# Which rows are kept, where raw weights lie and when gathers begin in a two-layer encoder with a product-key expert layer

## The chip, the cores and the metric

The kernel runs on one core of a Trainium2 chip. The metric is device time in microseconds of one execution; runs of a kernel are told as their median. The profile is of one execution, taken by the hardware profiler.

## The reference, cut

Two layers act on 512 tokens of width 1024. Each layer has a mixing part (retention and dilated attention), a cross-attention to 256 memory tokens, and an expert layer. Only the expert layer is touched by the change:

```python
def block(xb):                                   # 128 tokens
    q = (xb @ w_query).reshape(128, 8, 2, 128)
    half_scores = jnp.einsum('thcd,ckd->thck', q, keys_f)          # 2 x 128 keys a head
    top_s, top_i = lax.top_k(half_scores, 16)
    cand_s = top_s[:, :, 0, :, None] + top_s[:, :, 1, None, :]
    cand_i = top_i[:, :, 0, :, None] * 128 + top_i[:, :, 1, None, :]
    best_s, best_pos = lax.top_k(cand_s.reshape(128, 8, -1), 16)
    expert_idx = jnp.take_along_axis(cand_i.reshape(128, 8, -1), best_pos, axis=-1)
    gates = jax.nn.softmax(best_s, axis=-1)
    u, v = expert_down[expert_idx], expert_up[expert_idx]          # 16384 experts of width 1024
    act = jax.nn.gelu(jnp.einsum('thkd,td->thk', u, xb))
    return jnp.einsum('thk,thkd->td', gates * act, v)
```

So each token uses 8 x 16 = 128 of 16384 experts. All is in float32.

## The kernel before

The 512 tokens are four blocks of 128, numbered 0 to 3. The kernel computes the expert layer in two ways. For blocks 0 to 2 (`ND` = 384 tokens) it is *dense*: all 16384 experts are multiplied out, and a gate array `Gd` in DRAM, zero where an expert wasn't chosen, selects. For block 3 it is *sparse*: the 128 rows that each token chose are gathered from DRAM, one slot for all 128 tokens at a time.

The dense part goes over 128 groups (`i1`) of 128 experts. `Dense.down` loads a group's down weights into a `w_raw` tile (512 KB, on the queue of SyncE, SP), splits it into a high part `w_hi` (ScalarE, line 106) and a low part `w_lo` (VectorE, line 107), does 24 matmuls of 128 x 384 into the PSUM tile `pj` (line 658; 8 steps of three products of the parts), and ScalarE writes the gelu of it as a tile `c`. `up_parts` loads the group's up weights in the same way, multiplies `c` with the gates (VectorE, line 688) and splits it into `ch` and `cl`; `up` does 18 matmuls of 128 x 512 (line 700) into six accumulators that fill six banks of PSUM for the whole stage. `w_raw` has four tiles (`WR`) for both kinds of weights.

The sparse part issues an indirect DMA on GpSimd's queue for each of 128 slots (line 560), first from the down table, where VectorE takes a dot product of each row with the token (line 565), then from the up table, where VectorE adds the weighted row to `x` (line 571). A gathered tile is 512 KB, and `RB` = 3 of them exist.

A `Route` object holds a block's choice: `sv` and `si` are the top-16 scores and indices of each half (written by `top16` in `tail`, while the query projection runs), `half` combines them for four heads (VectorE mostly; ScalarE's exponential in it is line 793), `gates` builds one-hot rows (VectorE, lines 836 to 850), multiplies them on TensorE (lines 859 and 860) and writes `Gd`. Tiles of Routes 0 and 2 share names (`sv0`), and so a buffer; Route 1 has `sv1`, and Route 3 has a set of its own in the pool `layer`.

`layer` writes the order of the program with generators. For the expert layer it is:

1. Eight steps, each with one piece of the second pair's query projection (`t1`), three steps of the choices of Routes 0 and 1, and two downs whose `c` is put away in DRAM (`Cd`), since the PSUM that the ups need is still in use. Such blocks are the *kept* ones.
2. The rest of the choices of Routes 0, 1 and 2, with two downs a step, then downs until `LAG` = 60 are kept (blocks 0 to 59).
3. `rest`: blocks 60 to 127, each with its down and its up; after each, the ups of as many kept blocks as fall due, whose `c` is read back as `cd` (three tiles). Gate tiles are loaded eight blocks at a time (1536 KB), as `gt` for the blocks with a down and as `gtb` for the kept ones, two tiles each. Beside it run Route 3's two halves and the 256 gathers, 262 steps spread over the 68 blocks.

This program order is then handed to a scheduler (`schedule_with_timeline_sim`), which sets each engine's order and the waits; each engine and each queue works in that order.

Of the kernel before, what the change touches and what calls it, by code (L numbers as in the profile page):

```python
# [8 lines left out]
F32 = mybir.dt.float32  # L9
# [12 lines left out]
D = 1024  # L22
# [5 lines left out]
NK = 128  # L28
NE = NK * NK
SLOTS = 128  # L30
# [5 lines left out]
GSC = 4096.0  # L36
ND = 384
# [15 lines left out]
WR = 4  # L53
KH = 7
AH = 5
FP = ((0, 0, 0), (0, 1, 1))
SIDE = 262


class Kernel:  # L60
# [67 lines left out]

    def wload(self, src):
        raw = self.wp.tile([128, D], F32, name="w_raw", bufs=WR)  # L130
        self.nc.sync.dma_start(raw if len(src.shape) == 2 else raw.rearrange("p (a b) -> p a b", a=src.shape[1]), src)
        return raw

    def wsplit(self, src, pool=None):

        raw = self.wload(src)
# [307 lines left out]
    def tail(self, l, pair, pools, gp, lp):  # L444

        nc, a, ps = self.nc, self.a, self.ps
        sb = pools["tail"]
# [7 lines left out]
        hT = operand(FP[pair][0], "P_lo")  # L455
# [49 lines left out]
        self.bcast_rows(gain, a["norm_ffn"], l * D, D)  # L505
        d = 2 * pair * 128
        inner = d + 256 <= ND
        if inner:
            hT = [t[:, :, d:d + 256] for t in self.hT]
        else:  # L510
            hT = pools["hq"].tile([128, KT, 256], F32, name="hq"),
        keep = {}
        for i in range(2):
            b = 2 * pair + i
            if b * 128 >= ND:
                keep[i] = self.hn[b] = lp.tile([128, D], F32, name=f"hn{b}")
        for i, h in self.norm_rows(sb, xs, gain, keep, ("a4", A4)):
            b = 2 * pair + i
            self.to_T(h, hT, i * 128, self.hT if b * 128 < ND and not inner else None, b * 128)
        yield  # L520
# [30 lines left out]

    def sparse(self, b, r, gp, lp):
        nc, a = self.nc, self.a
        ei = r.ei
        act = lp.tile([128, SLOTS], F32, name=f"act{b}")
        c = lp.tile([128, SLOTS], F32, name=f"cf{b}")

        def gather(tab, j):
            t = gp.tile([128, D], F32, name="row", bufs=RB)
            nc.gpsimd.indirect_dma_start(out=t, out_offset=None, in_=tab,  # L560
                                         in_offset=bass.IndirectOffsetOnAxis(ap=ei[:, j:j + 1], axis=0))
            return t
        for j in range(SLOTS):
            t = gather(a["expert_down"], j)
            nc.vector.scalar_tensor_tensor(t, t, 1.0, self.hn[b], op0=OP.mult, op1=OP.mult, accum_out=act[:, j:j + 1])  # L565
            yield
        nc.scalar.activation(c, act, AF.Gelu_apprx_tanh)
        nc.vector.tensor_mul(c, c, r.g)
        for j in range(SLOTS):
            t = gather(a["expert_up"], j)  # L570
            nc.vector.scalar_tensor_tensor(self.x[b], t, c[:, j:j + 1], self.x[b], op0=OP.mult, op1=OP.add)  # L571
            yield

    def layer(self, l):
        nc, a = self.nc, self.a
        with ExitStack() as lst:
# [3 lines left out]
            dp = self.pool(lst, "gdram", space=DRAM)  # L580
            self.hn, self.routes = {}, []
            self.Gd = dp.tile([ND // TB, 128, NK, TB], F32, name="Gd")
# [31 lines left out]
            def sparse():  # L614
                for r in self.routes:
                    if r.b * 128 >= ND:
                        r.sb = late
                        yield from r.half(0)
                        yield from r.half(1)
                        r.rows(lp)  # L620
                        yield from self.sparse(r.b, r, late, lp)
            dense.rest(late, sparse())

# [10 lines left out]
class Dense:  # L634
# [3 lines left out]
    def __init__(self, k, l, sb, dp):  # L638
        self.k, self.l, self.sb = k, l, sb
        self.nb = ND // 128  # L640
        self.gview = k.Gd.rearrange("n p i t -> p n i t")
        self.Cd = dp.tile([LAG, 128, ND], F32, name="Cd")
        self.acc, self.started = {}, set()
        self.n = 0
# [19 lines left out]
    def ahead(self, n):  # L664

        for i1 in range(self.n, min(self.n + n, LAG)):
            self.k.nc.scalar.dma_start(self.Cd[i1], self.down(i1))
            self.n = i1 + 1

    def kept(self, i1):  # L670
        c = self.late.tile([128, ND], F32, name="cd", bufs=3)
        self.k.nc.sync.dma_start(c, self.Cd[i1])
        return c

    def gates(self, pool, i1, name, bufs):

        if i1 % GI == 0 or name not in self.gt:
            t = self.gt[name] = pool.tile([128, ND // TB, GI, TB], F32, name=name, bufs=bufs)
            i0 = i1 // GI * GI
            self.k.nc.sync.dma_start(t, self.gview[:, :, i0:i0 + GI, :])  # L680
        return self.gt[name][:, :, i1 % GI, :]

# [20 lines left out]

    def rest(self, pool, side):

        k, nb = self.k, self.nb
        for b in range(nb):
            self.bank(b)
        self.gt, self.late = {}, pool
        owed = 0.0  # L710
        kept = 0
        last = []

        def add(parts, i):
            if i < NK - 2:
                self.up(parts, 0, nb)
            else:
                last.append(parts)
        n = 0
        for i1 in range(LAG, NK):  # L720
            add(self.up_parts(self.down(i1), self.gates(pool, i1, "gt", 2), i1), n)
            n += 1
            while kept < LAG and kept * (NK - LAG) < (i1 + 1 - LAG) * LAG:
                add(self.up_parts(self.kept(kept), self.gates(pool, kept, "gtb", 2), kept), n)
                kept += 1
                n += 1
            owed += SIDE / (NK - LAG)
            take(side, int(owed))
            owed -= int(owed)
        take(side, 1000)  # L730
        for b in range(nb):
            self.up(last[0], b, b + 1)
            self.up(last[1], b, b + 1, True)
            for h in range(2):
                x = k.x[b][:, h * 512:(h + 1) * 512]
                k.nc.vector.tensor_add(x, self.acc[b, h], x)


class Route:


    def __init__(self, k, l, b, sb, lp):
        self.k, self.l, self.b, self.sb = k, l, b, sb
        i = b % 2
        if b * 128 >= ND:
# [59 lines left out]
    def rows(self, lp):  # L805

        self.ei = lp.tile([128, SLOTS], I32, name=f"ei{self.b}")
        self.k.nc.vector.tensor_scalar(self.ei, self.ef, float(self.l * NE), None, op0=OP.add)

    def gates(self):  # L810
# [18 lines left out]
        def pairs(x, t, n):  # L829

            return x[:, t:t + n].rearrange("p (o t) -> p o t", t=TP)[:, :, None]

        def same(out, j, t):
            n, m = out.shape[1] * TP, out.shape[2]
            v = [128, n // TP, m, TP]
            nc.vector.tensor_tensor(out, k.iota_r[:, None, 0:m, :].to_broadcast(v), pairs(iT[:, j], t, n).to_broadcast(v),
                                    op=OP.is_equal)
        no = OB // TP
        for t0 in range(0, 128, OB):
# [11 lines left out]
            for t1 in range(0, OB, TB):  # L851
# [3 lines left out]
                for q in range(0, TB, 4):  # L855
# [5 lines left out]
                    nc.scalar.activation(stage[:, :, q:q + 4], pg.rearrange("p t i -> p i t"), AF.Copy, scale=1.0 / GSC)  # L861
                nc.scalar.dma_start(k.Gd[(self.b * 128 + t0 + t1) // TB], stage)
# [62 lines left out]
```

## Time and profile before

| | |
|---|---|
| median of 3 runs | 3653.78 us (3647.8 to 3661.69) |
| the profiled execution | 3647.1 us, span 3645.3 us |
| TensorE (PE) busy | 3501.8 us, 96% |
| VectorE (DVE) busy | 2651.4 us, 73% |
| ScalarE (ACT) busy | 1481.2 us, 41% |
| GpSimd (POOL) busy | 640.9 us, 18% |
| DMA, mean over the span | 848.42 MB, 233 GB/s |

Layer one's `rest` runs from about 965 to 1822 us of the span, layer two's from about 2786 to 3626. The rows of a table by stretches give, after the stretch and its length, the busy time of PE, PE's weight loads (PEld), DVE, ACT and POOL with the number of instructions in brackets, then the clock that TensorE was granted (1.00 is full), the busy share of the 16 DMA engines, and GB/s. A row of waits says who stood idle at which line for whom: total us, times, longest. "SPq" is SyncE's DMA queue; q1 in the list of queues is that queue, q10 ScalarE's, q0 GpSimd's. Matmuls overlap in the pipeline, so that the time from one start to the next, and not the duration of one, is what a matmul costs.

### The profile page before, as it was taken

The page shows a single profiled execution, that of the slowest core. Times are in us where ns is not written, and L with a number is a line of the kernel's source. Part 1 is how long each engine was busy: PE and PEld are TensorE (multiplying, and loading weights), DVE is VectorE, ACT ScalarE, POOL GpSimd, SP SyncE. Part 2 cuts the span into 40 slices and gives each one's busy share as a digit, 9 for nine tenths or more (in the row PEclk, how much of TensorE's full clock was granted, in tenths as well). Part 3 has the DMA queues.
Part 4 walks back from the last instruction along what each step waited for, and adds up shares of the span by engine and source line. Part 5 has one row for each costly group of instructions (what it writes and reads, how often), then busy time and mean ns, then how long its engine had stood idle before and what let it go on. Part 6 is the DMA issues. An engine that isn't in the chain of part 4 may idle for free.

```text
span 3645.3 us, 55355 instructions
## 1 busy us (share of the span) xinstructions
PE 3501.8 (96%) x20844; PEld 3190.9 (88%) x20844; DVE 2651.4 (73%) x5818; ACT 1481.2 (41%) x2214; POOL 640.9 (18%) x518
## 2 busy tenths in 40 slices
PE   8999999999899999999989999999998999999997
PEld 7989989999788888888779899899997888888886
DVE  5565559976677777878855655599766777878787
ACT  4453544454433333333333535345544333333332
POOL 0000000000133433434300000000000333333342
PEclk9999999999999999999999999999999999999998
DMA  5242444666799989998832434346668999999986
GB/s 158 77 135 94 152 127 148 221 227 229 250 318 326 331 313 325 332 320 308 306 96 77 129 105 152 122 150 219 230 226 253 333 329 327 328 325 338 325 311 237
DMA packets 432252, 848.42 MB, mean 233 GB/s; under 512 B 27888, under 2 KB 282864, under 8 KB 425840
## 3 DMA queue, kind: packets, MB, share of 16 engines
q1 hardware_dynamic: 326384, 489.89, 41.2%
q0 software_dynamic: 73728, 268.47, 20.8%
q10 hardware_dynamic: 31872, 86.52, 6.6%
q8 instruction: 163, 2.67, 0.3%
q14 instruction: 105, 0.86, 0.1%
HBM read 756.17 MB, written 76.02 MB: 228 GB/s over the span
## 4 chain that ended last, share of the span: by engine, by line
PE 55%; issue 14%; DMA 12%; DVE 9%; POOL 7%; ACT 2%; SPq 1%; POOLq 0%; DVEq 0%; ACTq 0%
PE pj L658 16%; PE pj L167 13%; PE pj L183 9%; DMA row<-in_expert_up,ei 7%; POOL row L560 7%; PE s L700 2%; PE t L700 2%; DVE w_lo L107 2%; DMA w_raw<-in_down_T 2%; DVE x L571 2%; DMA row<-in_expert_down,ei 1%; PE o L700 1%; PE g L700 1%; PE s L338 1%; PE g L346 1%
## 5 line engine op out<-in xcount | busy, mean ns | idle before, releaser
L106 ACT ACTIVATE w_hi<-w_raw 128x1024 fp32r<-128x1024 f32 x696 | 732.3, 1059 | 1007.5 <-PE g L700 324.5
L107 DVE TENSOR_TENSOR w_lo<-w_raw,w_hi 128x1024 fp32r<-128x1024 f32 x696 | 848.0, 1222 | 379.4 <-ACT w_hi L106 355.1
L560 POOL DMA_INDIRECT row<-in_expert_down,ei x256 | 315.0, 1231 | 2498.1 <-DMA cd<-Cd 1981.2
L658 PE MATMUL pj<-hT_hi,w_hi 128*128 128x384 f32 x2048 | 699.0, 341 | 26.5 <-ACT w_hi L106 19.0
L658 PE MATMUL pj<-hT_hi,w_lo 128*128 128x384 f32 x2048 | 696.2, 340 | 5.3 <-DVE w_lo L107 5.3
L658 PE MATMUL pj<-hT_lo,w_hi 128*128 128x384 f32 x2048 | 700.4, 342 | 0.0
L658 PEld LDWEIGHTS pj<-hT_hi,w_hi 128*128 128x128 f32 x2048 | 386.9, 189 | 37.2 <-ACT w_hi L106 21.0
L560 POOL DMA_INDIRECT row<-in_expert_up,ei x256 | 325.3, 1271 | 474.9 <-DVE x L571 403.8
L658 PEld LDWEIGHTS pj<-hT_hi,w_lo 128*128 128x128 f32 x2048 | 386.6, 189 | 11.7 <-DVE w_lo L107 7.9
L571 DVE SCALAR_TENSOR_TENSOR x<-row,cf,x 128x1024 f32<-128x1024 f32 x256 | 328.1, 1282 | 93.5 <-DMA row<-in_expert_up,ei 92.4
L658 PEld LDWEIGHTS pj<-hT_lo,w_hi 128*128 128x128 f32 x2048 | 386.6, 189 | 6.7
L565 DVE SCALAR_TENSOR_TENSOR row<-row,hn 128x1024 f32<-128x1024 f32 x256 | 311.6, 1221 | 85.1 <-DMA row<-in_expert_down,ei 84.7
L106 ACT ACTIVATE ch<-c 128x384 fp32r<-128x384 f32 x136 | 71.5, 526 | 344.6 <-DVE c L688 287.3
L700 PE MATMUL s<-w_hi,ch 128*128 128x512 f32 x512 | 165.1, 404 | 44.1 <-ACT ch L106 44.0
L661 ACT ACTIVATE c<-pj 128x384 f32<-128x384 f32 x256 | 123.1, 481 | 129.0 <-PE pj L658 107.5
L700 PE MATMUL s<-w_lo,ch 128*128 128x512 f32 x512 | 162.1, 398 | 1.9 <-DVE w_lo L107 1.8
L700 PE MATMUL t<-w_hi,ch 128*128 128x512 f32 x512 | 163.4, 397 | 0.0
L700 PE MATMUL t<-w_lo,ch 128*128 128x512 f32 x512 | 162.6, 398 | 0.0
L183 PE MATMUL pj<-w_hi,T_hi 128*128 128x256 f32 x640 | 156.9, 286 | 3.8 <-ACT w_hi L106 2.7
L700 PE MATMUL s<-w_hi,cl 128*128 128x512 f32 x512 | 159.3, 392 | 0.0
L700 PE MATMUL t<-w_hi,cl 128*128 128x512 f32 x512 | 158.6, 391 | 0.0
L167 PE MATMUL pj<-T_hi,w_hi 128*128 128x512 f32 (+1 forms) x512 | 149.0, 341 | 1.8 <-DVE qlo L253 1.8
(259 smaller groups left out, 7254.9 us busy)
## 6 DMA issues: line engine op xcount, KB each, us to landing
w_raw<-in_down_T SPq DMA_DIRECT2D x256, 512.0 KB, 5.1
w_raw<-in_expert_up SPq DMA_DIRECT2D x256, 512.0 KB, 5.8
Gd<-mq ACTq DMA_DIRECT2D x48, 1024.0 KB, 6.3
w_raw<-in_peer_w_query SPq DMA_DIRECT2D x64, 512.0 KB, 3.7
w_raw<-in_w_in SPq DMA_DIRECT2D x56, 512.0 KB, 4.1
gt<-Gd SPq DMA_DIRECT2D x18, 1536.0 KB, 13.4
gtb<-Gd SPq DMA_DIRECT2D x16, 1536.0 KB, 13.8
Cd<-c ACTq DMA_DIRECT2D x120, 192.0 KB, 2.9
```

Of the source, the lines that this page charges most:

```text
L106: self.nc.scalar.activation(hi, src, AF.Copy)
L107: self.nc.vector.tensor_sub(lo, src, hi)
L167: nc.tensor.matmul(ps[:, :T], wt[k // 4][x][:, k % 4, s * 128:(s + 1) * 128], hT[y][:, k, :T], start=(k == 0 and x == y), stop=(k == KT - ...
L183: nc.tensor.matmul(ps[:, :256], hT[x][:, k, ts], wt[k // 4][y][:, k % 4, :], start=(k == 0 and x == y), stop=(k == KT - 1 and (x, y) == pa ...
L338: nc.tensor.matmul(s, ks[i][:, kb * 128:(kb + 1) * 128], q, start=(i == 0), stop=(i == 1))
L346: nc.tensor.matmul(po[:, qb, :], pts[kb][:, qb * 128:(qb + 1) * 128], rv[:, kb, h * HD:(h + 1) * HD], start=(kb == 0), stop=(kb == NB - 1))
L560: nc.gpsimd.indirect_dma_start(out=t, out_offset=None, in_=tab, in_offset=bass.IndirectOffsetOnAxis(ap=ei[:, j:j + 1], axis=0))
L565: nc.vector.scalar_tensor_tensor(t, t, 1.0, self.hn[b], op0=OP.mult, op1=OP.mult, accum_out=act[:, j:j + 1])
L571: nc.vector.scalar_tensor_tensor(self.x[b], t, c[:, j:j + 1], self.x[b], op0=OP.mult, op1=OP.add)
L658: k.nc.tensor.matmul(pa[:, :ND], x[:, kk, :], y[:, kk, :], start=(kk == 0 and x is dh and y is hi), stop=(kk == KT - 1 and x is dl))
L661: k.nc.scalar.activation(c, pa[:, :ND], AF.Gelu_apprx_tanh)
L700: self.k.nc.tensor.matmul(self.acc[b, h], cc[x][:, s], uu[y][:, h * 512:(h + 1) * 512], start=(b, h) not in self.started, stop=last and x ...
```

## The change

- The kept blocks are the last four of every eight, 64 in all (`KEPT`), and `rest` goes over the groups of eight in order: one block with its down, then a kept one, four times. One gate tile `gt` serves both; `gtb` is gone.
- Up weights have raw tiles of their own (`UR` = 4, in the pool `late`), beside the four in the old pool. Kept rows read back have five tiles, gathered rows four (`RB`).
- Route 3's halves and the first gathers move ahead of `rest`: after five steps of Route 2's choice, with two downs each, come Route 3's two halves, and then each further iteration (two downs, and a step of Route 2's gates while there are any) takes three gathers (`SROWS`). The remaining ones are spread evenly over `rest` (`left`).
- The gathered rows and the tiles of the sparse part move to the pool `dense`; Route 3's `sv`, `si` and `ef` share Route 1's.

```diff
-LAG = 60
+KEPT = [i for i in range(NK) if i % 8 > 3]
+SROWS = 3
-RB = 3
+RB = 4
+UR = 4
-SIDE = 262
...
     def wload(self, src, pool=None):
+        raw = (pool or self.wp).tile([128, D], F32, name="w_raw", bufs=UR if pool else WR)
...
-            side = chain(side, *[r.choose() for r in self.routes[2:] if r.b * 128 < ND])
-            while next(side, side) is not side:
+            rows = self.sparse(self.routes[SP], dense.sb)
+            left = 2 * SLOTS
+            take(side, 1000)
+            side = self.routes[2].choose()
+            for _ in range(5):
+                take(side, 1)
                 dense.ahead(ROWS)
-            dense.ahead(LAG)
+            take(rows, 5)
+            while next(side, side) is not side or dense.n < len(KEPT):
+                dense.ahead(ROWS)
+                take(rows, SROWS)
+                left -= SROWS
             ost.close()
             gst.close()
-            late = self.pool(lst, "late")
...
-            dense.rest(late, sparse())
+            dense.rest(self.pool(lst, "late"), rows, left)
...
+    def gates(self, pool, g):
+        t = pool.tile([128, ND // TB, GI, TB], F32, name="gt", bufs=2)
+        self.k.nc.sync.dma_start(t, self.gview[:, :, g * GI:g * GI + GI, :])
+        return t
...
-        for i1 in range(LAG, NK):
-            add(self.up_parts(self.down(i1), self.gates(pool, i1, "gt", 2), i1), n)
-            n += 1
-            while kept < LAG and kept * (NK - LAG) < (i1 + 1 - LAG) * LAG:
-                add(self.up_parts(self.kept(kept), self.gates(pool, kept, "gtb", 2), kept), n)
-                kept += 1
-                n += 1
-            owed += SIDE / (NK - LAG)
-            take(side, int(owed))
-            owed -= int(owed)
+            owed += left / (NK - 4)          # in add(), after each block's up
+            take(side, int(owed))
+            owed -= int(owed)
+        kept = {i1: j for j, i1 in enumerate(KEPT)}
+        for g in range(NK // GI):
+            gt = self.gates(pool, g)
+            group = range(g * GI, g * GI + GI)
+            for pair in zip([i for i in group if i not in kept], [i for i in group if i in kept]):
+                for i1 in pair:
+                    c = self.kept(kept[i1]) if i1 in kept else self.down(i1)
+                    add(self.up_parts(c, gt[:, :, i1 % GI, :], i1))
...
 class Route:
-        if b * 128 >= ND:
-            i, sb = b, lp
```

More of the change, by code (lines that the diff above doesn't have):

```diff
@@ L36 @@
 GSC = 4096.0
-ND = 384
+SP = 3
+DB = (0, 1, 2)
+ND = 128 * len(DB)
 TB = 16
@@ L127, in parts, with wload @@
             self.nc.scalar.activation(o[0], src, AF.Copy)
-    def wload(self, src):
-        raw = self.wp.tile([128, D], F32, name="w_raw", bufs=WR)
+    def wload(self, src, pool=None):
+        raw = (pool or self.wp).tile([128, D], F32, name="w_raw", bufs=UR if pool else WR)
         self.nc.sync.dma_start(raw if len(src.shape) == 2 else raw.rearrange("p (a b) -> p a b", a=src.shape[1]), src)
@@ L134, in wsplit @@
     def wsplit(self, src, pool=None):
-        raw = self.wload(src)
+        raw = self.wload(src, pool)
         hi = (pool or self.wp).tile([128, D], F32R, name="w_hi", bufs=2 if pool else 3)
@@ L505, in tail @@
         self.bcast_rows(gain, a["norm_ffn"], l * D, D)
-        d = 2 * pair * 128
-        inner = d + 256 <= ND
+        blocks = 2 * pair, 2 * pair + 1
+        inner = SP not in blocks
         if inner:
+            d = DB.index(blocks[0]) * 128
             hT = [t[:, :, d:d + 256] for t in self.hT]
@@ L512, in tail @@
         keep = {}
-        for i in range(2):
-            b = 2 * pair + i
-            if b * 128 >= ND:
-                keep[i] = self.hn[b] = lp.tile([128, D], F32, name=f"hn{b}")
+        if not inner:
+            keep[SP - blocks[0]] = self.hn = lp.tile([128, D], F32, name="hn")
         for i, h in self.norm_rows(sb, xs, gain, keep, ("a4", A4)):
-            b = 2 * pair + i
-            self.to_T(h, hT, i * 128, self.hT if b * 128 < ND and not inner else None, b * 128)
+            b = blocks[i]
+            both = not inner and b != SP
+            self.to_T(h, hT, i * 128, self.hT if both else None, DB.index(b) * 128 if both else 0)
         yield
@@ L549, in top16, with sparse @@
         nc.vector.max_index(idx[:, 8:16], v[:, 8:16], wk)
-    def sparse(self, b, r, gp, lp):
+    def sparse(self, r, sb):
         nc, a = self.nc, self.a
-        ei = r.ei
-        act = lp.tile([128, SLOTS], F32, name=f"act{b}")
-        c = lp.tile([128, SLOTS], F32, name=f"cf{b}")
+        yield from r.half(0)
+        yield from r.half(1)
+        ei = r.rows(sb)
+        act = sb.tile([128, SLOTS], F32, name="act")
+        x = self.x[r.b]
         def gather(tab, j):
-            t = gp.tile([128, D], F32, name="row", bufs=RB)
+            t = sb.tile([128, D], F32, name="row", bufs=RB)
             nc.gpsimd.indirect_dma_start(out=t, out_offset=None, in_=tab,
@@ L641, in __init__ @@
         self.gview = k.Gd.rearrange("n p i t -> p n i t")
-        self.Cd = dp.tile([LAG, 128, ND], F32, name="Cd")
+        self.Cd = dp.tile([len(KEPT), 128, ND], F32, name="Cd")
         self.acc, self.started = {}, set()
@@ L664, in ahead, with kept @@
     def ahead(self, n):
[L666 to L672, printed above, removed]
-        return c
[L675 to L681, printed above, removed]
+        for j in range(self.n, min(self.n + n, len(KEPT))):
+            self.k.nc.scalar.dma_start(self.Cd[j], self.down(KEPT[j]))
+            self.n = j + 1
+    def kept(self, j):
+        c = self.late.tile([128, ND], F32, name="cd", bufs=5)
+        self.k.nc.sync.dma_start(c, self.Cd[j])
+        return c
+    def gates(self, pool, g):
+        t = pool.tile([128, ND // TB, GI, TB], F32, name="gt", bufs=2)
+        self.k.nc.sync.dma_start(t, self.gview[:, :, g * GI:g * GI + GI, :])
+        return t
     def up_parts(self, c, g, i1):
@@ L702, in up, with rest @@
                     self.started.add((b, h))
-    def rest(self, pool, side):
+    def rest(self, pool, side, left):
         k, nb = self.k, self.nb
@@ L708, in rest, with add @@
             self.bank(b)
[L709 to L715, printed above, removed]
+        self.late = pool
+        owed, n, last = 0.0, 0, []
+        def add(parts):
+            nonlocal owed, n
+            if n < NK - 2:
                 self.up(parts, 0, nb)
@@ L744, in __init__ @@
         i = b % 2
-        if b * 128 >= ND:
-            i, sb = b, lp
         self.sv = sb.tile([128, 8, 2, 16], F32, name=f"sv{i}")
@@ L805, in rows @@
     def rows(self, lp):
-        self.ei = lp.tile([128, SLOTS], I32, name=f"ei{self.b}")
-        self.k.nc.vector.tensor_scalar(self.ei, self.ef, float(self.l * NE), None, op0=OP.add)
+        ei = lp.tile([128, SLOTS], I32, name="ei")
+        self.k.nc.vector.tensor_scalar(ei, self.ef, float(self.l * NE), None, op0=OP.add)
+        return ei
     def gates(self):
@@ L835, in same @@
             v = [128, n // TP, m, TP]
-            nc.vector.tensor_tensor(out, k.iota_r[:, None, 0:m, :].to_broadcast(v), pairs(iT[:, j], t, n).to_broadcast(v),
-                                    op=OP.is_equal)
+            nc.vector.tensor_tensor(out, k.iota_r[:, None, 0:m, :].to_broadcast(v),
+                                    pairs(iT[:, j], t, n).to_broadcast(v), op=OP.is_equal)
         no = OB // TP
@@ L861, in gates @@
                     nc.scalar.activation(stage[:, :, q:q + 4], pg.rearrange("p t i -> p i t"), AF.Copy, scale=1.0 / GSC)
-                nc.scalar.dma_start(k.Gd[(self.b * 128 + t0 + t1) // TB], stage)
+                nc.scalar.dma_start(k.Gd[(DB.index(self.b) * 128 + t0 + t1) // TB], stage)
                 yield
```

22 lines of the change are left out of this document (7 added, 15 removed).

## The prediction

> **What bounds the kernel now.** I read the page first, then the busy time by stage, then the waits of the last stage, then the gathers' own tile and the queues.
>
> ```profile
> span 3645.3 us, 55355 instructions
> PE 3501.8 (96%) x20844; PEld 3190.9 (88%) x20844; DVE 2651.4 (73%) x5818; ACT 1481.2 (41%) x2214; POOL 640.9 (18%) x518
> PE 55%; issue 14%; DMA 12%; DVE 9%; POOL 7%; ACT 2%; SPq 1%; POOLq 0%; DVEq 0%; ACTq 0%
> ```
>
> PE is busy for 96% of the span, yet the chain that ended last is only 55% PE: the rest runs through gathers and the engines that use them. All sums below are against this execution, 3647.1 us (span 3645.3). The median of the runs is 3653.8, 6.7 higher; I add 6.7 at the end.
>
> The change touches two stages of each layer: "ahead" (downs with no gather beside them) and "rest" (downs, ups, gathers). By stage:
>
> ```profile
> core 0: us, PE busy (x) PEld busy (x) DVE busy (x) ACT busy (x) POOL busy (x), PEclk, DMA share, GB/s
> 800.00:937.00 137.00, 137.00 (x1002) 133.45 (x1001) 74.37 (x153) 63.41 (x101) 0.00 (x0) 1.00 0.69 233
> 937.00:975.00 38.00, 25.14 (x112) 22.57 (x111) 23.77 (x102) 13.72 (x17) 0.00 (x0) 0.82 0.90 257
> 975.00:1785.00 810.00, 781.67 (x3718) 685.22 (x3717) 630.93 (x812) 280.47 (x374) 313.06 (x247) 0.99 0.92 318
> 2765.00:2803.00 38.00, 25.66 (x101) 22.42 (x100) 25.32 (x90) 17.41 (x21) 0.00 (x0) 0.78 0.72 221
> 2803.00:3605.00 802.00, 780.48 (x3734) 685.46 (x3733) 633.30 (x812) 280.18 (x374) 310.99 (x252) 0.99 0.93 326
> ...
> 830.00:840.00 10.00, 10.00 (x59) 10.00 (x58) 1.00 0.64 218
> ...
> 1405.44 1.36 PE s L700 x6
> 1406.81 1.36 PE t L700 x6
> ```
>
> The row with x59 is line 658 alone: undisturbed, a down matmul starts every 10/58.7 = 0.170 us, so a down (24) costs 4.09 us. An up matmul starts every 1.36/6 = 0.227 us, so an up (18) costs 4.08. The rest has 68 downs and 128 ups: 278 + 522 = 800 us for 3936 matmuls, 0.2035 each. Against that, PE loses time in three places. In ahead: nothing, 137 busy of 137. At the transition (937 to 975): 112 matmuls are worth about 22 us of 38; 16 lost, 18 in layer two, with the granted clock down to 0.82 and 0.78. In the rest: 3718 x 0.2035 = 757 of 810, 53 lost; 3734 x 0.2035 = 760 of 802, 42 lost. Together 69 and 60 us a layer, 129 in all. That is the ceiling of the gain, since the change removes no matmul.
>
> Who makes PE lose it, layer one:
>
> ```profile
> DVE x L571 <- DMA row<-in_expert_up,ei: 51.0, 40, 3.6
> DVE row L565 <- DMA row<-in_expert_down,ei: 47.7, 38, 3.7
> DVE cd L688 <- DMA cd<-Cd: 26.2, 15, 7.9
> ACT w_hi L106 <- DMA w_raw<-in_down_T: 118.4, 35, 12.2
> SPq L131 <- DVE w_lo L107: 476.6, 172, 9.6
> ...
> 1030.40 5.79 SPq L131 DMA_DIRECT2D w_raw<-in_down_T  x1
> ...
> 1046.02 1.06 ACT L106 ACTIVATE w_hi<-w_raw 128x1024 fp32r<-128x1024 f32 x1 [5.53 <-DMA w_raw<-in_down_T]
> ```
>
> DVE, which works in order, stands 99 us before gathered rows and 26 before kept rows, with the w_lo and gate products of the next block behind it. The SP queue stands 477 us until w_lo (line 107) gives back one of four raw tiles that downs and ups share. The last two rows are one case: a down's load takes 5.8 us to get through its queue, and ScalarE then stands 5.5 us until the data are there.
>
> ```profile
> L560 POOL DMA_INDIRECT row<-in_expert_down,ei x256: 935/1015/1977, 986.6 to 3216.8; - x128
> L565 DVE SCALAR_TENSOR_TENSOR row<-row,hn x256: 1214/1220/1228, 991.6 to 3226.4; 128x1024 f32<-128x1024 f32 x128
> DMA to landing us min/median/max: 4.2/6.7/10.6
> ...
> L571 DVE SCALAR_TENSOR_TENSOR x<-row,cf,x x128: 1269/1280/1289, 1418.2 to 1817.3; 128x1024 f32<-128x1024 f32 x128
> ```
>
> 256 gathers from 987 to 1817 are one each 3.24 us; with three row tiles a tile's round is 9.7 us, of which 1.0 (issue), 6.7 (landing) and 1.3 (DVE) = 9.0 are needed. So the ring of gathers is as full as PE is: two bounds side by side, each disturbing the other.
>
> **The change, part by part.**
>
> *Kept downs 60 to 64, every kept block beside one that is not kept.* Four downs move from rest to ahead: 4 x 4.09 = 16.4 us later start, 16.4 less afterwards: 0. Four more kept rows, each written and read back (4 x 0.39 MB), stand against one gate tile fewer (17 loads to 16, 1.57 MB each): the DMA moves the same.
>
> *Row tiles 3 to 4, 57 gathers moved out of the rest.* 19 iterations of two downs (26 to 64) take three gathers each, so 199 of 256 remain. In the rest a gather is then due every 785/199 = 3.9 us (floor 64 x 4.09 + 128 x 4.08 = 784) and four tiles give a round of 15.8 us for the 9.0 needed: the wait of DVE for rows should nearly go. The DVE loses 57 x 1.22 = 70 us of 631 there, the DMA 57 x 0.524 = 30 MB of 318 GB/s x 810 us = 258 (a gather is 128 rows of 4 KB).
>
> *Raw tiles 4 to 4 + 4, kept rows 3 to 5.* A down's load no longer stands behind an up's tile in use; its bound is 0 to the whole rest loss, together with the gathers. What SP is then late with is only the gate tile every eight blocks. Together: of the rest's loss, 53 + 42 = 95 us, I take two thirds away, 63 (ends 0 and 95): the three waits named, for rows, for kept rows and for raw tiles, all get slack, but the DMA stays near its ceiling (B, below), so I do not take it all.
>
> *Route 3's halves (its choice of experts) run in ahead; the gate load has 22 downs between the last gate and the rest* (eight of the 19 iterations carry a gate step, 11 x 2 downs follow). Now the transition holds these halves, a 1.57 MB load of gt and one of gtb, and the first loads for the ups, all at once; PE's chain hangs on the first of them:
>
> ```profile
> 944.62 10.25 DMA gt<-Gd
> ```
>
> I take away two thirds of the 16 + 18: 23 us (ends 0 and 34). What is late next is the first up's weights, behind the gate load in SP's queue.
>
> *What ahead pays.* PE is full there, so any wait is a loss. Queues now:
>
> ```profile
> q1 hardware_dynamic: 5316, 14.89, 37.7%
> q10 hardware_dynamic: 5485, 16.89, 30.9%
> ...
> q1 hardware_dynamic: 74848, 128.47, 46.3%
> q0 software_dynamic: 35302, 128.56, 45.1%
> ```
>
> The first two are 800 to 937, the others 975 to 1785. From 800 on PE needs 137 us, plus the 4 new downs and some two still open at 937 (an estimate from 38 us in which PE did 22 us of work): 6.3 x 4.09 = 26, so 163 us. DMA: 31.8 MB, less 2.8 MB of loads for the rest (one gate tile, two ups, one kept row), plus 6.3 x 0.72, plus 30 of gathers = 63.5 MB. The stages moved 318 GB/s at a share of 0.92 and 233 at 0.69, so a full share is some 342: 186 us, 23 more than PE. At the 326 GB/s that layer two's rest really held, 195, 32 more. DVE: 74 + 70 for the gathers + at most 24 for the halves (the transition's whole DVE time) + 5 for the new downs' w_lo (four of 1.2) = 173, 10 more than PE. The DVE is in order, so a late row holds the next w_lo and PE dries up. Ends 0 (the scheduler lets gathers slide into the rest) and 32; I take 23, the DMA's, a layer: +46.
>
> By the Trainium skill ("DMA: Bandwidth & Descriptors", Specifications) the limit of a core is about 358 GB/s; the 63.5 MB would then take 177 us and ahead would pay 14 a layer, 18 us less in all. No stretch of a whole stage here moved more than 326.
>
> Sum: -63 - 23 + 46 = -40: 3607 on this execution, 3614 as a median.
>
> **The rivals.**
>
> *A, forecast: rest and transition gain more than ahead pays.* Gain 20 to 75, so 3579 to 3634.
>
> *B, no change.* Ahead pays its full 32 a layer (64) and the rest gets only half of its loss back (48): its stretch still has 258 - 30 - 2 = 226 MB in 757 - 16 = 741 us of PE work, 305 GB/s, a share of 0.89 against 0.92. With 23 from the transition that is -7: 3647. For it: the same gathers, ups and downs go through the same queues at nearly the ceiling over both stages. Against: PE, not DMA, is full in the best stretches.
>
> *C, slower: the query projection waits for a tile.* Route 3's sv and si had tiles of their own and now share Route 1's. So no top-16 of Route 3 can be written until Route 1's second half has run:
>
> ```profile
> 679.16 0.26 ACT L793 ACTIVATE gd<-gd 128x64 f32<-128x64 f32 x1 [1.62 <-DVE gd L792]
> ...
> 600.00:620.00 20.00, 10.95 (x51) 9.47 (x50) 1.00 0.52 161
> 700.00:720.00 20.00, 7.50 (x32) 5.90 (x32) 1.00 0.68 245
> ...
> 600.00:727.00 127.00, 126.67 (x862) 118.53 (x861) 126.12 (x554) 63.20 (x93) 0.00 (x0) 1.00 0.59 203
> ```
>
> Route 1's second half, the fourth of a layer's eight, ran at 679, while the projections that feed Route 3 (line 167 alone, the two rows of 20 us) ran from before 600 to past 700, and DVE was full all through (126 of 127). If DVE does Route 1's halves first, PE fills with downs, which cost nothing later; if projections pile up in both pj banks, PE stands for up to 679 - 600 = 79 us, say 40 a layer: +80 - 40, 3694. It decides from 20 a layer, and from 29 the kernel is measurably slower. Against: Route 2 already shares Route 0's tiles in this way and PE shows no gap.
>
> *D, ahead costs nothing.* If rows reach PE's loads first, gathers are late but only they. In the rest q0 and q1 had nearly equal shares, 45.1 and 46.3%; with three queues a third of 342 GB/s is 114, and 34 downs' 17.8 MB take 156 us, within PE's 163. Then -63 - 23 = -86: 3568. It needs DVE's order to leave w_lo ahead of the late rows. By the Trainium skill ("DMA: Bandwidth & Descriptors", Queues, rings and completion order) each DMA engine goes round the queues that have work, packet by packet; the equal shares in the rest agree with it.
>
> **How the numbers follow.** A 0.50, D 0.13, B 0.21, C 0.16. Within 0.5% (18 us, about what a measurement of this kernel can tell) is 3636 to 3672. Faster: A and D, 0.63; same: B, 0.21; slower: C, 0.16. The time is A's, 3614; A's own range is 3579 to 3634. The range for 8 in 10 goes from D's 3568, a little lower for its own uncertainty, 3564, to the edge of C, 3672.
>
> **What would show it.** Right: gathers start near 800 and 2630, 57 of them before the first up; PE matmuls from 975 on at 0.205 to 0.21 us instead of 0.218; DVE's waits for rows under 30 us a layer; no clock dip at the transition; in ahead PE loses 10 to 30 us and the DMA share is above 0.9. Wrong: PE idle between 600 and 727 with the wait on line 757 to 759 or 545 (C); ahead longer than 200 us from 800 on, or SP's waits for w_lo in the rest as long as now (B); ahead with PE full (D).

## The result, and the profile after

The changed kernel takes 3559.4 us (median of four runs, 3558.6 to 3560.8) against 3650.8 for the kernel before: 0.977 of it, 95% interval 0.974 to 0.979. The forecast was 3614 with a range from 3564. The sign was right, the gain twice as large as the sum had it: on the profiled executions the span went from 3645.3 to 3558.2, 87 us less, where the terms gave 40.

The page's first lines and the head of its chain of waits, changed kernel:

```profile
span 3558.2 us, 55460 instructions
PE 3475.2 (98%) x20844; PEld 3181.1 (89%) x20844; DVE 2649.6 (74%) x5818; ACT 1472.7 (41%) x2214; POOL 698.9 (20%) x518
PE 88%; DVE 7%; DMA 2%; ACT 1%; issue 1%; SPq 0%; ACTq 0%; DVEq 0%
```

Each of the five engines runs as many instructions as before. The chain that ended last was 55% PE and is now 88%.

To place the 87 us, I cut each layer at three points: its first down matmul, its first up matmul, its last up matmul. The first stretch is ahead and the transition, the second the rest. The busy time by stretches, kernel before (first down to first up, first up to last up, for each layer):

```profile
589.70:965.30 375.60, 362.44 (x2526) 347.51 (x2525) 290.56 (x1013) 180.43 (x270) 0.00 (x0) 0.99 0.67 224
965.30:1820.60 855.30, 824.08 (x3903) 721.73 (x3904) 669.01 (x877) 298.79 (x397) 324.54 (x256) 0.99 0.91 315
...
2409.70:2785.80 376.10, 363.40 (x2527) 348.49 (x2526) 290.59 (x1013) 180.37 (x270) 0.00 (x0) 0.99 0.67 224
2785.80:3627.90 842.10, 820.58 (x3904) 719.98 (x3905) 664.60 (x874) 296.68 (x394) 315.78 (x256) 0.99 0.90 316
```

The same, changed kernel:

```profile
589.10:986.40 397.30, 387.55 (x2659) 371.41 (x2658) 347.38 (x1133) 195.20 (x287) 49.43 (x37) 0.99 0.73 268
986.40:1770.40 784.00, 784.00 (x3777) 692.43 (x3776) 611.85 (x758) 279.56 (x381) 296.60 (x219) 1.00 0.90 317
...
2360.40:2759.00 398.60, 388.98 (x2662) 372.58 (x2661) 348.30 (x1134) 195.26 (x286) 49.34 (x37) 0.99 0.73 267
2759.00:3544.60 785.60, 783.40 (x3773) 691.86 (x3773) 610.06 (x769) 278.10 (x378) 302.92 (x219) 1.00 0.88 311
```

The brackets behind PE count its matmuls. The first stretch now holds 133 and 135 more of them, downs at 0.170 us: 22.6 and 23.0 us of work, and it is 21.7 and 22.5 us longer. So it costs 1.4 us less than before. The second stretch is 71.3 and 56.5 us shorter; 126 and 131 matmuls fewer are 21.4 and 22.3 us of that, so 84 us are real. Both layers together: 83.6 us by the lengths alone; the 2 us between are most likely matmul records that the trace lacks. What is left, 3.5 us, lies behind the last up (17.4 us before, 13.6 now). So the gain is the rest's alone. PE was idle there for 31.2 and 21.5 us before, and for 0.0 and 2.2 now, which is 50 of the 84. The other 34 don't show as idle time: by the prediction's prices (a down 4.09 us, an up 4.08) the two rests had lost 61 + 47 = 108 us before, and lose 11 + 13 now.

The waits of the rest, changed kernel, in the order in which the prediction showed them:

```profile
DVE cd L691 <- DMA cd<-Cd: 26.2, 10, 4.8
...
ACT w_hi L109 <- DMA w_raw<-in_down_T: 8.6, 3, 3.2
...
DVE x L578 <- DMA row<-in_expert_up,ei: 4.8, 5, 2.2
...
DVE row L572 <- DMA row<-in_expert_down,ei: 2.9, 4, 1.3
```

and SP's queue:

```profile
SPq L134 <- DVE w_lo L110: 479.2, 162, 12.5
```

VectorE's 99 us before gathered rows are 8, ScalarE's 118 before raw down weights 9. VectorE's wait for kept rows is as long as before (26.2), although they have five tiles instead of three. SP stands as long as before until w_lo gives a raw tile back (476.6, then 479.2), and PE doesn't suffer from it now. The prediction took a wait as long as before for a sign of "no change"; here it was no sign of either.

### The profile page after: what moved, and what is told of

It is laid out like the page before. It is cut to its first block, busy times and chain, and to the rows that moved or that the text cites. A ratio compares the mean times of both kernels' runs of the same rounds, so it can differ in the third digit from the quotient of the medians.

```text
span 3558.2 us, 55460 instructions
## 1 busy us (share of the span) xinstructions
PE 3475.2 (98%) x20844; PEld 3181.1 (89%) x20844; DVE 2649.6 (74%) x5818; ACT 1472.7 (41%) x2214; POOL 698.9 (20%) x518
## 4 chain that ended last, share of the span: by engine, by line
PE 88%; DVE 7%; DMA 2%; ACT 1%; issue 1%; SPq 0%; ACTq 0%; DVEq 0%
PE pj L663 27%; PE pj L170 12%; PE s L703 10%; PE t L703 10%; PE pj L186 10%; PE o L703 5%; PE g L703 5%; DVE w_lo L110 1%; DMA w_raw<-in_down_T 1%; PE s L341 1%; PE g L349 1%; PE o L349 1%; PE t L380 1%; PE s L371 1%; PE g L387 1%
## 5 line engine op out<-in xcount | busy, mean ns | idle before, releaser
L566 POOL DMA_INDIRECT row<-in_expert_down,ei x256 | 338.2, 1321 | 2313.5 <-PE pj L663 923.6
L566 POOL DMA_INDIRECT row<-in_expert_up,ei x256 | 360.1, 1407 | 452.7 <-DVE x L578 413.1
L578 DVE SCALAR_TENSOR_TENSOR x<-row,act,x 128x1024 f32<-128x1024 f32 x256 | 327.4, 1279 | 6.8 <-DMA row<-in_expert_up,ei 5.4
L572 DVE SCALAR_TENSOR_TENSOR row<-row,hn 128x1024 f32<-128x1024 f32 x256 | 309.3, 1217 | 17.5 <-DMA row<-in_expert_down,ei 17.4
L109 ACT ACTIVATE ch<-cd 128x384 fp32r<-128x384 f32 x128 | 66.7, 521 | 232.7 <-PE g L703 227.6
```

What stands on the lines that cost most here:

```text
L109: self.nc.scalar.activation(hi, src, AF.Copy)
L572: nc.vector.scalar_tensor_tensor(t, t, 1.0, self.hn, op0=OP.mult, op1=OP.mult, accum_out=act[:, j:j + 1])
L578: nc.vector.scalar_tensor_tensor(x, t, act[:, j:j + 1], x, op0=OP.mult, op1=OP.add)
```

## The experiments

### Rival C: Route 3 with tiles of its own

`x4`: one line more in `Route.__init__`.

```diff
         i = b % 2
+        if b == SP:
+            i, sb = b, lp
```

> The changed kernel, but Route 3's sv, si and ef have tiles of their own again, as before the change. Theory C (the query projection waits until Route 1's second half has freed the shared tile): the PE gap near 600 us of layer one (5.5 busy of 10 us) and near 2370 of layer two goes, and the kernel gains 8 to 14 us: 3545 to 3552. Rival (the gap is only work that moves, because VectorE is full there anyway): within 4 us of 3559.

Measured: 3539.3 us, 0.971 [0.967, 0.975] of before, and 19 us less than a repeat of the changed kernel on the same chip (`x1`, below). The gap that it closes, changed kernel, two stretches, and the wait in the timeline (start, duration, engine, line, operation, in brackets the idle time before it):

```profile
600.00:610.00 10.00, 5.54 (x28) 4.60 (x27) 9.57 (x47) 5.80 (x8) 0.00 (x0) 1.00 0.39 129
610.00:620.00 10.00, 10.00 (x53) 9.98 (x52) 9.79 (x50) 5.44 (x7) 0.00 (x0) 0.83 0.21 70
...
609.47 0.49 PE L539 MATMUL s<-keysT,b 128*128 128x128 f32 x2 [4.46 <-ACT b L533]
...
606.66 1.06 ACT L109 ACTIVATE w_hi<-w_raw 128x1024 fp32r<-128x1024 f32 x1 [3.77 <-DMA w_raw<-in_down_T]
```

PE, in order, stands at the score matmul of a query projection (line 539) for 4.5 us, and the clock that it is granted in the next 10 us is 0.83. It waits for ScalarE's copy of the projection (line 533), and ScalarE had itself stood 3.8 us for a raw down weight; VectorE is full (9.57 of 10). No wait in this chain names the shared tile. That the tile is at its start follows from the runs: from 600 to 630 PE is busy for 25.1 to 25.6 us of 30 in every run in which Route 3 shares Route 1's tiles, and for 30.0 in every run in which it doesn't. In `x4`, its first down to first up in each layer:

```profile
591.10:981.40 390.30, 387.29 (x2670) 371.44 (x2669) 347.91 (x1134) 194.43 (x285) 52.79 (x40) 1.00 0.76 271
...
2352.20:2742.80 390.60, 387.52 (x2669) 371.73 (x2668) 348.25 (x1135) 194.54 (x285) 52.51 (x40) 1.00 0.76 271
```

By the same count as above (144 and 142 more matmuls than before, 24.5 and 24.1 us, in 14.7 and 14.5 us more) this stretch gains 19.4 us against before, where the changed kernel gains 1.4. So the shared tiles cost 18 us, 9 a layer. Some 9 of the 18 are the two gaps themselves (4.5 us, and 4.3 near 2380), and some 4, by an estimate, the lower clock behind them (5 us at 0.66 and 5 us at 0.50). Another 4 are PE's idle time at the transition, 4.7 and 5.1 us in the changed kernel (the next two rows; layer two's from 2720 to 2765) against 2.7 and 2.7 in `x4`:

```profile
940.00:990.00 50.00, 45.33 (x242) 42.98 (x241) 29.02 (x39) 17.18 (x23) 9.97 (x9) 0.97 1.04 380
2720.00:2765.00 45.00, 39.94 (x208) 37.23 (x207) 26.62 (x37) 16.84 (x23) 9.14 (x8) 0.96 1.00 371
```

So rival C's mechanism is there, in the stretch that it named though not with a wait on the lines that it named, at a quarter of its price of 40 a layer.

`x8`: `x4` with six raw tiles for up weights, `UR = 6`.

> x4 with six raw tiles for up weights in place of four. If the loss left at the start of the rest (PE 47.3 busy of 50 us, layer one) is a wait for up weights, it gains 3 to 8 us: 3531 to 3536. If it is the DMA itself, which moves 358 GB/s there: within 3 us of x4's 3539.

3546.9 us, 0.972 [0.968, 0.975]: no gain. `x4` took the least time of all versions; `x8` ran on another chip, and by the ratio to before the two are equal.

### What ahead pays, and whether the DMA bounds the rest

`x1`: the gathers of ahead left to `rest`.

```diff
-                take(rows, SROWS)
-                left -= SROWS
```

> The changed kernel, but no gather is issued beside the downs ahead: all 256 are spread over the rest; Route 3's halves, the raw tiles, four row tiles and the order of blocks stay. Theory G (the gain comes from taking 57 gathers out of the rest, whose DMA was near its ceiling): the rest has to move 30 MB more a layer in about 785 us, 375 GB/s, which it can't, so at 340 GB/s it takes some 40 us longer a layer and the kernel goes back to about 3630 us (3610 to 3645). Theory R (the gain comes from separate raw tiles and more row and kept-row tiles, so that no load stands behind another): PE stays full in the rest, at most 20 us are lost, 3560 to 3580.

3558.3 us, 0.977 [0.973, 0.980]. A miss: its gathers begin at 840.3 us as in the changed kernel, a microsecond after their indices are written (839.1): the scheduler has drawn them forward, and their place in the program did not hold them back. It is the changed kernel over again, and tells nothing of the question.

`x5`: as `x4`, but the gathered rows lie in the pool `late`, which opens with the rest, so that none can start earlier; Route 3's halves run in the rest, too.

```diff
-            rows = self.sparse(self.routes[SP], dense.sb)
-            left = 2 * SLOTS
+            left = 2 * SLOTS + 5
...
-            take(rows, 5)
...
-                take(rows, SROWS)
-                left -= SROWS
...
-            dense.rest(self.pool(lst, "late"), rows, left)
+            late = self.pool(lst, "late")
+            self.routes[SP].sb = late
+            dense.rest(late, self.sparse(self.routes[SP], late), left)
```

> As x4 (Route 3 with own tiles), but now Route 3's two halves and the row tiles too lie in the rest's pool, so that no gather can start before the rest, as before the change; raw tiles, four row tiles, five kept-row tiles and the order of blocks stay. In x1 the gathers began near 840 us all the same, because the scheduler places them as soon as their tiles and indices are there, so x1 did not test theory G. Theory G (early gathers matter): the rest has to move some 375 GB/s against the 337 of x1, falls short by 20 to 40 us a layer, and the transition holds the halves again: 3580 to 3625 us. Theory R (only the tiles matter): within 10 us of x4, 3535 to 3550.

3559.1 us, 0.975 [0.972, 0.978]. Two stretches of its rests:

```profile
990.00:1700.00 710.00, 710.00 (x3428) 628.24 (x3428) 578.42 (x753) 254.05 (x345) 300.12 (x228) 1.00 0.97 342
...
2765.00:3470.00 705.00, 705.00 (x3402) 623.39 (x3401) 574.32 (x747) 250.62 (x339) 301.42 (x225) 1.00 0.97 341
```

All 256 gathers run in the rest, from 987 on, and PE is busy for 710 of 710 and 705 of 705 us. So with the tiles of the change the DMA load of the rest is not its bound, and moving gathers out of it relieves nothing there. Without these tiles it is otherwise (`x9` and `x10`, below). What `x5` loses against `x4` (15 us by the spans, 3554.2 and 3539.0) lies behind the last up: from there to the next layer's first down 597.5 us (1765.5 to 2363.0) against 588.9 (1763.3 to 2352.2), and 18.6 to the end of the span (3535.6 to 3554.2) against 14.3. Its last gathered row is added at 3536.2, after the last up; that of `x4` at 3477.5, 47 us ahead of it. So what early gathers still pay here is that they are done in time.

The DMA in ahead, changed kernel, three stretches and the queues of the first of them (packets, MB, share of 16 engines' span):

```profile
840.00:940.00 100.00, 100.00 (x739) 97.28 (x738) 79.53 (x140) 44.65 (x73) 40.28 (x29) 1.00 0.98 374
850.00:900.00 50.00, 50.00 (x390) 48.40 (x389) 48.47 (x95) 23.09 (x39) 18.83 (x14) 1.00 1.01 389
2650.00:2700.00 50.00, 50.00 (x380) 48.55 (x380) 39.95 (x69) 23.16 (x38) 19.30 (x13) 1.00 1.01 396
...
q0 software_dynamic: 4026, 14.67, 39.4%
q10 hardware_dynamic: 3980, 12.26, 30.4%
q1 hardware_dynamic: 2841, 10.33, 27.6%
```

The prediction's full share of 342 GB/s is passed by 9% over 100 us, and by up to 16% over 50, with PE full.

`x15`: `x4` with six gathers in each iteration of ahead, `SROWS = 6`.

> The changed kernel with tiles of its own for Route 3, and six gathers, not three, in each iteration of ahead: 114 there, not 57. If ahead pays nothing for gathers, as the runs so far have it: 3535 to 3545, PE full from 800 us to the last down. If the prediction's price was only put too high (VectorE or the DMA becomes the bound when the gathers are many): 57 x 1.22 = 70 us more of VectorE work in ahead than before, which must wait in part; PE then has gaps between 800 and 970 and the time is 3560 or more.

3557.5 us, 0.974 [0.971, 0.977]. Inconclusive for the price: from 800 to 990 GpSimd issued 41 operations, in `x4` 40, so the gathers didn't double. Their indices are written at 826 (`x4` 828), and from then on one is issued every 4 us in both; the order in the program did not set their number. So what 57 gathers in ahead would have cost was not measured. The 18 us more (by the spans) are partly at the transition: 940 to 990 in `x4`, then in `x15`:

```profile
940.00:990.00 50.00, 47.33 (x246) 44.92 (x245) 25.50 (x36) 16.11 (x24) 8.03 (x7) 0.97 1.00 358
```

```profile
940.00:990.00 50.00, 42.74 (x226) 41.61 (x225) 22.63 (x31) 13.99 (x20) 9.43 (x8) 0.93 1.02 360
```

PE loses 4.6 us more here and the granted clock falls to 0.93; layer two has the same (38.04 of 45 against 42.26). By the cuts used above, `x15` loses 10 us against `x4` up to the first ups, 7 in the two rests and 3 between the layers. From 990 to 1700 and from 2765 to 3470 PE is full in both; why the ends of `x15`'s rests are longer was not found.

### Which part brings the rest its gain

Parts alone. `x6`: the kernel before with four row tiles, `RB = 4`.

> The kernel before with four row tiles in place of three, nothing else. Theory ring: VectorE's waits for rows, 99 us in layer one's rest, fall below 40, and 20 to 30 us are gained: 3610 to 3630 us. Rival (the shared raw tiles and the full DMA hold the rest whatever the ring): under 10 us, 3635 to 3650.

3617.7 us, 0.992 [0.989, 0.994]: 34 us of gain from one tile.

`x12`: Route 3's halves and the first gathers ahead, in the order of the kernel before.

```diff
-            while next(side, side) is not side:
-                dense.ahead(ROWS)
-            dense.ahead(LAG)
...
+            for _ in range(7):
+                take(side, 1)
+                dense.ahead(ROWS)
+            take(rows, 5)
+            while next(side, side) is not side or dense.n < LAG:
+                dense.ahead(ROWS)
+                take(rows, 3)
+                left -= 3
...
```

> The kernel before, but Route 3's halves run ahead and the gathers may start there, as in the change; three row tiles, shared raw tiles, the old order and two gate streams stay. Theory S: a ring of three then has 11 us a round and more, the transition loses its halves, and most of x7's gain is there: 3575 to 3605 us. Theory O: under 30 us gained, 3622 to 3650.

3623.9 us, 0.992 [0.990, 0.995]: 28 us.

`x11`: the gather steps handed out after every block instead of every block with a down.

> The kernel before, but the gathers' steps are handed out after every block (2.1 each) instead of after every block with a down (3.9 each). If bunches of four gathers on three tiles were the wait (theory bunch): 20 to 35 us gained, 3615 to 3632. If the scheduler evens the bunches out by itself, as it moved the gathers of x1: within 10 us, 3640 to 3655.

3657.0 us, 1.001 [0.999, 1.004]: nothing.

`x9`: `x5` without any tile of the change (shared raw tiles, `RB = 3`, three kept-row tiles), so that the order with one common gate tile is left, on Route 3's own tiles and with the gathers in the rest.

> x5 (halves and gathers only in the rest, Route 3 with own tiles) with shared raw tiles, three row tiles and three kept-row tiles: what is left of the change is the order of blocks, the common gate tile and gathers spread over every block. Theory S (spacing: early gathers and the spread leave a ring of three enough slack, 11.8 us a round in x7 against 9.7 before): here 256 gathers in about 790 us give 9.3 us a round again, so the rest stalls as before and most of the gain is gone, 3620 to 3650 us. Theory O (the order of blocks and gate loads did it): it keeps at least half of x7's 79 us, 3580 to 3610.

3615.2 us, 0.990 [0.987, 0.993]: 37 us. Its transition and rest:

```profile
940.00:990.00 50.00, 49.98 (x267) 47.25 (x267) 38.97 (x108) 25.49 (x31) 7.54 (x7) 1.00 0.82 262
990.00:1700.00 710.00, 694.30 (x3314) 607.95 (x3313) 561.57 (x733) 251.12 (x335) 269.66 (x218) 0.99 0.95 332
```

PE has no gap at the transition, where it had 12.9 us before, and is idle for 15.7 us of the 710. One gate tile to load there instead of two is the likeliest reason; it was not tried alone.

`x7`: the changed kernel without its extra tiles, so order and early gathers together; `x10`: the same with Route 3's own tiles.

```diff
-RB = 4
+RB = 3
...
-        raw = (pool or self.wp).tile([128, D], F32, name="w_raw", bufs=UR if pool else WR)
+        raw = self.wp.tile([128, D], F32, name="w_raw", bufs=WR)
...
-        c = self.late.tile([128, ND], F32, name="cd", bufs=5)
+        c = self.late.tile([128, ND], F32, name="cd", bufs=3)
```

> The changed kernel with shared raw tiles, three row tiles and three kept-row tiles: what is left is the order of blocks, the common gate tiles and the early halves and gathers. If the two effects of x2 (38 us) and x3 (28 us) add up: 3559 + 66 = 3625 us. If either wait takes the place of the other (each alone hides the other's): 3595 to 3610. If the tiles are all of the gain: 3640 to 3655. Theory G says that early gathers keep a good part: below 3620.

> x7 (no extra tiles) with Route 3's own tiles. If the shared tile costs the same 20 us here as between the changed kernel and x4, it is independent of the rest: 3549 to 3557. If it overlaps with the rest's waits: 3560 to 3573.

3572.8 us, 0.978 [0.975, 0.982], and 3570.6, 0.979 [0.976, 0.981]. So order and early gathers together bring 79 us; the tiles add some 14 by the medians, though the intervals overlap. Taken by the times alone, 79 isn't clearly more than 37 + 28, given the intervals; the places of the gains tell more. One profiled execution of each run, cut as above, gives these gains over before in us, both layers together (`x9`'s execution is its slowest, 10 us above its median):

| | ahead and transition | rest |
|---|---|---|
| `x6`, fourth row tile alone | 0 | 33 |
| `x12`, early halves and gathers alone | 27 | 2 |
| `x9`, order alone | 29 | 9 |
| `x7`, order and early gathers | 14 | 59 |
| `x10`, the same, own tiles | 21 | 50 |
| changed kernel | 1 | 84 |
| `x4`, the same, own tiles | 19 | 87 |

The same in the middle of layer one's rest, before, `x12`, `x7` and the changed kernel:

```profile
990.00:1700.00 710.00, 687.37 (x3279) 603.76 (x3278) 549.20 (x718) 244.80 (x326) 273.80 (x216) 0.99 0.93 323
...
990.00:1700.00 710.00, 688.04 (x3287) 603.60 (x3286) 549.00 (x685) 245.09 (x328) 280.52 (x214) 0.99 0.93 322
...
990.00:1700.00 710.00, 704.60 (x3390) 621.75 (x3389) 568.87 (x710) 256.75 (x339) 277.93 (x220) 1.00 0.94 334
...
990.00:1700.00 710.00, 710.00 (x3427) 627.94 (x3426) 577.91 (x718) 253.90 (x345) 295.78 (x219) 1.00 0.96 337
```

Alone, the order and the early gathers each gain at the transition, and next to nothing in the rest. Together they gain 59 there. `x9` and `x10` differ only in whether Route 3's halves and the first gathers come early: 9 us in the rest against 50, and 3615.2 against 3570.6 in time. So early gathers are worth 45 us where there are no extra tiles, and some 15 where there are (`x5` and `x4`, by the spans). Why they need the new order was not shown. In `x10` the gap near 609 is closed, too (PE 30.0 of 30 from 600 to 630), and ahead and the transition gain 7 us over `x7`, but its rests lose 9, so that the time stays the same; this too stays open.

Parts taken out of the changed kernel singly. `x2`: up weights in the shared raw tiles (the second pair of lines above alone). `x3`: `RB = 3` alone. `x13`: both. `x14`: three kept-row tiles alone.

> The changed kernel, but downs and ups share the four raw tiles again. Theory R: SP's loads stand behind each other again, PE loses 20 to 40 us a layer in the rest, 3600 to 3640 us. Theory G: less than 8 us a layer, 3560 to 3575.

> The changed kernel with three row tiles in place of four. A gather is due every 3.9 us, three tiles give a round of 11.8 us for some 9.8 needed (1.0 + 7.5 + 1.3). Theory ring (the fourth tile frees VectorE of its waits for rows): waits for rows come back to 50 us a layer or more and the kernel loses 20 to 40 us, 3580 to 3600. Theories G and R without the ring: under 10 us, 3560 to 3569.

> The changed kernel with shared raw tiles and three row tiles, the kept rows' five tiles left. Theory 1 (the kept rows' five tiles flood ScalarE's queue and the others then need their own extra tiles): far slower than the changed kernel, by 38 us (as shared raw tiles alone) to 66 (38 + 28), so 3597 to 3625. Theory 2 (raw and row tiles must be in balance with each other, the kept rows' tiles don't matter): about as with no extra tiles, 3565 to 3580.

> The changed kernel with three tiles for kept rows read back, not five. Theory 1 (five kept tiles flood): same as or faster than the changed kernel, 3545 to 3560. Theory 2 (kept tiles don't matter): 3553 to 3565. A rival, that they are needed as the raw and row tiles are: VectorE's waits for kept rows rise and the time is 3575 or more.

| of before's time | own up tiles | shared raw tiles |
|---|---|---|
| four row tiles | 0.977 [0.974, 0.979] | `x2` 0.987 [0.983, 0.991] |
| three row tiles | `x3` 0.984 [0.980, 0.988] | `x13` 0.980 [0.977, 0.983] |

In us: `x2` 3597.0, `x3` 3587.2, `x13` 3577.4. `x14` takes 3569.3 us, 0.978 [0.974, 0.981], 10 more than the changed kernel: the kept-row tiles are worth little, and with them left in, `x13` is as fast as `x7`. So the first theory (they flood a queue) falls. (By the ratios to before `x14` loses only 3, and PE is full in its rests.) Either of the other two kinds makes the kernel slower when it comes alone (`x2` clear of the intervals; those of `x3` and `x13` overlap, though the slowest `x13` run is 2 us faster than the fastest of `x3`) and faster when it comes second. Cut as above, ahead and the transition gain 1 us in `x2`, 3 in `x3` and 13 in `x13`, the rest 43, 55 and 59. So most of what `x3` loses against `x13`, and nearly half of what `x2` loses, lies ahead of the first up. For the rest the waits give a reason. `x2`, its rest in three stretches, the last add of a row, and a wait:

```profile
990.00:1250.00 260.00, 253.85 (x1217) 222.01 (x1215) 210.94 (x317) 92.04 (x122) 110.98 (x87) 1.00 0.97 343
1250.00:1640.00 390.00, 379.81 (x1821) 332.58 (x1822) 325.91 (x350) 137.04 (x183) 172.24 (x129) 1.00 0.97 341
1640.00:1700.00 60.00, 60.00 (x291) 53.01 (x290) 29.64 (x37) 21.10 (x28) 0.00 (x0) 1.00 0.66 203
...
L578 DVE SCALAR_TENSOR_TENSOR x<-row,act,x x128: 1272/1279/1334, 1266.3 to 1650.9; 128x1024 f32<-128x1024 f32 x128
...
PEld pj L663 <- DVE w_lo L110: 20.0, 12, 2.2
```

The last row is added at 1651 (changed kernel 1699), so the gathers run faster. While they run PE loses 16 us, standing before w_lo; when they are over it is full. The three-tile kernels are the other way round. `x3`, waits of the same stretch:

```profile
DVE cd L691 <- DMA cd<-Cd: 53.7, 22, 7.3
DVE x L578 <- DMA row<-in_expert_up,ei: 43.9, 41, 3.5
...
DVE row L572 <- DMA row<-in_expert_down,ei: 33.2, 29, 2.5
```

`x13`:

```profile
ACT w_hi L109 <- DMA w_raw<-in_down_T: 70.2, 37, 4.8
...
DVE cd L691 <- DMA cd<-Cd: 35.9, 20, 3.8
DVE x L578 <- DMA row<-in_expert_up,ei: 32.5, 27, 3.1
...
DVE row L572 <- DMA row<-in_expert_down,ei: 26.8, 21, 3.4
```

With more weights in flight (`x3`) rows and kept rows come later, 131 us of VectorE's time against 95, and no wait for weights shows; without (`x13`) the weights are late, 70 us, but on ScalarE, which has time. So in the rest it looks like the share of DMA that each ring can claim, but that is argued and not shown. The scheduler's order changes with each of these edits and may have a part in it, above all at the transition; this stays open.

## Why the prediction was wrong, step by step

**The reading of the bound was right.** PE was the engine to fill, its loss by the count of matmuls was the ceiling, and VectorE's and ScalarE's waits for rows and raw weights went with it. A fourth row tile alone gave back 33 us of the rest's loss (`x6`), order and early gathers together 59 (`x7`), all parts 84. That order or early gathers alone would give back next to nothing there (`x9`, `x12`) was not foreseen. SP's wait for w_lo, which the prediction counted among the causes, stayed as it was.

**"Of the rest's loss, 53 + 42 = 95 us, I take two thirds away, 63."** Measured 84, of 108 in the whole of the rest. The third was held back because "the DMA stays near its ceiling". `x5` shows that this was no bound: all gathers in the rest, 342 GB/s, PE 710 of 710.

**Transition, -23.** PE's idle time from first down to first up fell from 13.2 and 12.7 us to 9.8 and 9.6 in the changed kernel, where about half is now the new gap (near 609 and 2380), and to 3.0 and 3.1 in `x4`. The size was about right.

**"What ahead pays", +46, is the step that failed most.** With Route 3's own tiles, ahead and the transition together gained 19.4 us (`x4`): by PE's idle time the transition gained 20, so ahead paid nothing. Two errors made the 46. First, the number of gathers: the program writes 57 into ahead, but GpSimd's column above has 37 operations up to the first up (40 in `x4`). The prediction's own figures, with 20 gathers fewer, give 63.5 - 10.5 = 53 MB, at 342 GB/s 155 us, under PE's 163: no charge. VectorE's sum falls from 173 to 149, also under it. It named that end ("the scheduler lets gathers slide into the rest") and took the other. Second, the ceiling: GB/s over busy share isn't the rate at a full share. The shares of 0.92 and 0.69 that gave 342 stand beside 0.98 at 374 and 1.01 at 389 to 396 now. The Trainium skill ("Perfetto Trace Analysis", Roofline) says that 358 GB/s is a core's share when both cores of a pair load, and that a core alone can pull more, up to about 435 for its 16 DMA engines. The stretches at 374 to 396 agree with it; the prediction cited 358 as a core's limit, for another case than this kernel on one core.

**Rival C** was priced as a case of its own, 40 us a layer or nothing. It was 9 a layer and belonged in the sum as a term from 0 to 40: the row that it argued from (VectorE 126 of 127 us, projections on both sides of Route 1's half) was right. "Route 2 shares in this way and PE shows no gap" did not carry over to Route 3.

**Rival D** (ahead costs nothing, 3568) came closest: ahead paid nothing, as it said. Its reason held in part. The three queues did not get equal thirds (39.4, 30.4 and 27.6% from 840 to 940, SP's queue the least), and PE was full all the same; VectorE stood only 7.8 us before rows from 840 to 1000, so there were hardly any late rows to keep from w_lo. The range ended 5 us above the result, since it went to D's sum and a little below, and D too kept the two thirds. With the whole 95 taken, its low end would have been 32 lower. **Rival B** had both of its terms on the wrong side.

Measured terms: rest -84, ahead and transition -1 (+18 for Route 3's tiles, -19 without them), outside -3.5 (not foreseen); together -88.5 by this count, against 87 by the spans.

## What to carry to other kernels

When an engine is the bound and rings of tiles stall it, count what it loses by its number of matmuls, not by its idle time alone (84 us against 50 here). Take that whole loss as the likely gain, and hold some back for the DMA only where the trace shows a stretch in which that engine waits at that rate; GB/s divided by busy share is no ceiling. Where a scheduler orders the work, a step moved in the program is a wish: what lies where follows from when its inputs and tiles are free, so count it by that. Add tiles to rings that share queues together and try each with and without the other, since one ring alone can gain less than none, and say for each part in which stage it gains, since two parts can gain the same thing at one place and need each other at the next; and a tile that two users come to share is a term in the sum, however small.

## What the runs showed of the hardware

The busy share of the DMA engines doesn't say what room is left: with 0.92 the rest of before moved 318 GB/s, with 1.01 ahead now moves 396, and `x15`, from 940 to 990, has 1.02 at 360. After PE's gap of 4.5 us at 609 the next 10 us were granted a clock of 0.83, by an estimate from these two numbers 1.7 us of work on top of the gap's own length. In layer two the gap of 4.3 us was followed by 5 us at 0.50. So by the same estimate two gaps of some 9 us together cost some 4 us more by the clock.
